# Buffers of a streamed transformer program at other address distances, and a longer warm-up

## The chip, the cores and the metric

One core of one Trainium2 chip runs the whole program in one launch. The metric is the device time of that core in microseconds (us), lower is better.

## The reference

A small language-model stack on 256 tokens of width 1024, batch 1. Block 1 has two layers. Each norms x, multiplies it with `w_in` (1024 x 8216 columns), runs four token mixers in parallel (retention, a state space scan, gated linear attention, an mLSTM), gates and merges their outputs, and projects with `w_out`. The first layer is followed by a gated feed-forward network, the second by a mixture of eight experts, two for each token:

```
u = h @ w_in;  y_ret, y_ssd, y_gla, y_ml = mixers(u)
merged = sum(sigmoid(gates) * einsum('bsnv,nvd->bsnd', ybr, w_branch)); x += merged @ w_out
ffn(h)  = (silu(h @ w1) * (h @ w3)) @ w2           # 1024 -> 2816 -> 1024
moe(h)  = sum over the two best experts e of gate_e * ffn_e(h)
```

Block 2 has two layers of attention beside a pooling branch, each with a modulated norm, followed by a modulated feed-forward network of the same size. Everything is float32.

## The kernel before, in words

Every product with a weight is done in three passes. A weight chunk of 128 x 2048 is loaded by one DMA issued by SP into a raw buffer; `chunk` splits it in halves of 1024 columns into a high part (`wh`, a cast on ScalarE, line 342) and a low part (`wl`, a subtraction on VectorE, line 338), both of type float32r. The activations are split the same way (`hh` and `hl`, `yh` and `yl`, and so on). `mm3` (lines 344 to 349) then issues high x high (line 346), low x high (347) and high x low (348). Most matmuls stream 256 columns (the tokens) through a stationary tile of 128 x 128 weights; in `tmode` and in the experts it is the other way round: 256 or 512 columns of weights stream through a stationary tile of tokens. In the profile a matmul is written out<-moving,stationary (`mm<-hh,wh`), where `mm` and `sm` are tags of PSUM banks. Before each matmul TensorE loads its stationary tile (PEld); while one matmul streams, the weights of the next are loaded.

The program has eight phases in this order, each with a work pool of its own: mix0 (work0), ff0 (work1), mix1 (work2), moe1 (work3), att0, ffb0, att1, ffb1 (work4 to work7). Three pools last through the program: `pers` (x, `hh`, `hl`, small things), `ring` (three raw buffers, four `wh`, four `wl`) and PSUM. Some phases have more weight buffers of their own, `rawx`, `whx` and `wlx`, which take turns with those of the ring. The order of instructions on each engine comes from the scheduler of the tile framework, which works from its own estimates, except where `in_order` and `after` fix it.

SBUF addresses follow from the program: pools stand one behind another (pers, ring, the phase's work pool), and within a pool the tags stand in the order of their first use, each with all its buffers, each buffer rounded up to 32 bytes per partition. The buffers that feed the three passes are 2048, 4096 or 8192 bytes long, and a tile of 128 columns is 512 bytes, so all tiles of a tag have one address modulo 512. These are, before:

| pool | address modulo 512 |
|---|---|
| pers, ring | hh, hl 256; raw, wh, wl 64; rstd 256 |
| work0, work2 | gate, m2, u 416; yh, yl 96 |
| work1 | unh, unl 64; yh, yl, whx, wlx 128 |
| work3 | G, xgh, xgl 288; mgh, mgl, whx, wlx 128; myh, myl 384 |
| work4, work6 | unh, unl 0 to 480 (buffers of 2064 bytes); whx, wlx 192 |
| work5, work7 | unh, unl 128 to 352 (2064 bytes); yh, yl, whx, wlx 448 |

At the start of `run` eight float32 matmuls of 128 columns on a tile of ones keep TensorE busy while the first loads are under way (lines 1605 to 1607). `settle` fills `hh` and `hl` some 25 us into the program; `ipad` and `rw` are small tiles of the mixers' phases. `cos2` and `sin2` in pers are first used late in moe1.

Of the kernel before, what the change touches and what calls it, by code (L numbers as in the profile page):

```python
# [17 lines left out]
P = 128  # L18
T = 256
# [18 lines left out]
# chunks of 256 columns of w_in, in the order of their use  # L38
# [4 lines left out]
class Layout:  # L43
    """Columns of a packed [128, n] array."""
# [50 lines left out]
def constants():  # L95
    """Tables that follow from the shapes alone."""
# [62 lines left out]
def host_arrays(i):  # L159
    """The inputs, laid out for the program: nothing is computed from them."""  # L160
# [48 lines left out]
    def kcols(w, width=256):  # L209
        """[1024, C] -> [C / width, 128, 8 * width]"""  # L210
        return w.reshape(KD, P, -1, width).transpose(2, 1, 0, 3).reshape(-1, P, KD * width)

    def krows(w, nk=2):
        """[K, 1024] -> [K / (128 nk), 128, nk * 1024]"""
        return w.reshape(-1, nk, P, D).transpose(0, 2, 1, 3).reshape(-1, P, nk * D)
# [27 lines left out]
    def mcols(w):  # L243
        """[8, 1024, 2816]: ten chunks of (4 k, 512) and one of (8 k, 256) for each expert."""
        a = w[:, :, :2560].reshape(NE, 2, 4, P, 5, 512).transpose(0, 4, 1, 3, 2, 5).reshape(NE, 10, P, 2048)
        b = w[:, :, 2560:].reshape(NE, 8, P, 256).transpose(0, 2, 1, 3).reshape(NE, 1, P, 2048)
        return np.concatenate([a, b], 1).reshape(NE * 11, P, 2048)
# [5 lines left out]

class Prog:
    def __init__(self, tc, a, out, stop=None):
        self.tc, self.nc, self.a, self.out, self.stop = tc, tc.nc, a, out, stop
        self.n = 0
        self.set, self.loaded, self.tabled, self.holds = None, None, [], []

# [1 line left out]
    def tile(self, pool, shape, tag, dt=F32, bufs=None):  # L261
        self.n += 1
        return pool.tile(list(shape), dt, tag=tag, name=f"{tag}_{self.n}", bufs=bufs)
# [24 lines left out]
    def group(self, name):  # L288
        """The activations from here on use this set of tables."""
# [17 lines left out]
    def wait(self, *ins, late=False):  # L307
        """These splits (or the like) are not to go before what is more urgent, on their engines."""
# [15 lines left out]
    def in_order(self):  # L324
        """VectorE and ScalarE take what is traced here in its order."""
# [14 lines left out]
    def split(self, hi, lo, src):  # L340
        """src = hi + lo, each in the 12 bits that one pass of TensorE carries."""
# [13 lines left out]
    def slot(self, tag, n, dt=F32, where=None):  # L355
        """The next buffer of a ring: BASE of them last through the program, more[tag] are the phase's own."""
# [9 lines left out]
    def chunk(self, src, n=2048, where=None, cuts=1, spare=None):  # L366
        """A chunk of weights [128, n] from DRAM, in two halves of (hi, lo); spare: gives buffers [128, 512] instead of the ring's."""
# [20 lines left out]
    def ahead(self, cuts=1):  # L388
        """The first two chunks of the next phase."""
        self.first = [self.chunk(q, where="base", cuts=cuts) for q in self.next]  # L390

    def kmajor(self, halves, width):
        """[(hi, lo)] by k-tile, of a chunk [128, k, width]."""
# [6 lines left out]
    def wmode(self, ps, ws, xh, xl, ncol=2, start=True, stop=True):  # L400
        """ps[c, t] (+)= sum over k of w[k, c] x[k, t]."""
# [6 lines left out]
    def tmode(self, ps, ws, xh, xl):  # L408
        """ps[t, c] = sum over k of x[k, t] w[k, c], for both blocks of tokens."""
# [6 lines left out]
    def small(self, shape, tag, bufs=2):  # L416
        """A buffer that may outlive a phase's own."""
        return self.tile(self.pers, shape, tag, F32, bufs)

    def square_sums(self, n, scale=None, tag="mm", add=None):  # L420
        """Sums over channels of squares, on all partitions, from n pairs of tiles [128, 512] given one after another."""
# [30 lines left out]
    def half(self, banks, k):  # L452
        """Tile k of the eight in four banks of PSUM."""
        return banks[k // 2][:, k % 2 * T:k % 2 * T + T]

    def begin(self, g, shift=None, fin=None, alias=False):
        """Norms x once its update has come, tile by tile, and starts with the two chunks that are already here.

        Their products are with x * g, before the scale r by token is known: whoever reads them applies it; with a
        shift, the products' column T is the product with the shift. fin: the gain of a norm of x itself that comes  # L460
        before."""
# [38 lines left out]
        for k in range(KD):  # L500
            for q in range(2):
                for i in self.raw_step(out[q], first[q], k):
                    if k == KD - 1:
                        # the sums of squares come first
# [9 lines left out]
    def places(self, tags, W):  # L514
        """Where the products of a chunk go: two tiles of W columns, in one bank if they fit."""
# [12 lines left out]
    def raw(self, chunk, *tags):  # L528
        """More products with x * g."""
# [6 lines left out]
    def settle(self, r, urgent=None):  # L536
        """The normed x as the rest of the phase takes it. urgent: what goes before the first chunk that follows, which goes before this."""
# [45 lines left out]
    def conv(self, ps, wname, bname, j0, pad, r=None):  # L583
        """silu of the causal convolution of two tiles of channels; taps in w columns (tile, tap). r: a scale by token."""
# [18 lines left out]
    def scores(self, h, k, q, ps):  # L603
        """ps[j, (i of block 0 and 1 | i of block 1)] = k_j . q_i for a head in half h % 2 of tile h // 2."""
# [5 lines left out]
    def values(self, po, h, v, s, tile=None, vs=None):  # L610
        """po[v, i] of a head: sum over j of v[j] s[j, i]."""
# [6 lines left out]
    def row(self, src, r, ps):  # L618
        """A row of src [128, 256] on all partitions."""
        self.nc.tensor.matmul(ps, self.ident[:, r:r + 1].to_broadcast([P, P]), src, start=True, stop=True)  # L620

    def seg(self, rows, r, colT, h):
        """exp(rows[r + h, i] + colT[j]) where j <= i, as [j, (i of both blocks | i of block 1)]."""
# [10 lines left out]
    def headnorm(self, o, g, gate, extra=None):  # L634
        """(head norm of o) * g * gate; o [128, 512] in PSUM. extra: added to the mean of the squares."""
# [27 lines left out]
    def gla(self, sm, gq, gk, l):  # L663
        """The decayed scores of the gated linear attention, [j, 4 heads, 384]."""
# [22 lines left out]
        # block 0 to block 1  # L687
# [10 lines left out]
        # halves of ever smaller blocks  # L698
# [27 lines left out]
        # each token with itself  # L726
# [9 lines left out]
    def mixers(self, l):  # L736
# [22 lines left out]
        # columns that pass a silu  # L759
# [12 lines left out]
        # rows by head, and the inputs of the linear attention  # L772
# [9 lines left out]
        # softplus(z) for dt, softplus(-z) for the forget gates: max(+-z, 0) + log1p(exp(-|z|))  # L782
# [23 lines left out]
        # -acs and i - B by key, for its own block and for the next  # L806
# [9 lines left out]
        # the stabilizer of the mLSTM: m = B + M  # L816
# [11 lines left out]
        # rows that go to all partitions: acs by head, -M by head  # L828
        rw = self.w([P, T], "rw", bufs=1)
# [3 lines left out]
        # gated linear attention  # L833
# [13 lines left out]
        # mLSTM  # L847
# [22 lines left out]
        # h = num / d, so that its norm is num / sqrt(mean num^2 + eps d^2)  # L870
        y_ml = self.headnorm(po, lambda t: self.par("mlg" + g, t), None, extra=d2)

        # state space
# [27 lines left out]
        # retention  # L901
# [29 lines left out]
        # gates and branches  # L931
# [20 lines left out]
        for i, (n, y) in enumerate(order[:3]):  # L952
            gates = []
            for dp in range(4):
                ps, gt = gate(n, dp)
                if i == 0:
                    # the sigmoid with the tables that are loaded: exp(-log(1 + exp(-x)))
# [25 lines left out]
        # the last one the other way round, so that the merged tiles come one after another  # L983
# [30 lines left out]
    def ffn(self, w1, w3, w2, begun, shifted=False, filler=0):  # L1014
        """(silu(h w1) * (h w3)) w2, in four banks of PSUM, two tiles of 128 columns in each."""
# [15 lines left out]
        for f in range(nfp):  # L1031
# [33 lines left out]
            # filler steps, evenly  # L1065
# [15 lines left out]
    def route(self, ps, rg):  # L1081
        """Ranks of the tokens in the lists of their experts, and their gates: [token, block, expert].

        ps: the logits, each still to be scaled by its token's rg[:, :, 0]; the gates go behind that."""
# [10 lines left out]
        # how many experts come before: with a larger logit, or with the same one and a smaller number  # L1095
# [16 lines left out]
        def rest():  # L1112
            """The gates, and how many tokens the fullest list has."""
# [25 lines left out]
    def gather(self, sel, rank, rg, iota, meanwhile=None):  # L1139
        """The tokens of the ranks in iota as columns, the way back, and their scales and gates, rg(block) by token."""  # L1140
# [17 lines left out]
        if meanwhile is not None:  # L1158
            # no weights before the tokens
# [53 lines left out]
    def gated(self, cx, py):  # L1213
        """The expert's output for its tokens, times their gates, split."""
# [8 lines left out]
    def scatter(self, cx, ys):  # L1223
        """x += ys, each row to its token."""
# [8 lines left out]
    def tokens(self, dp):  # L1233
        """Two tiles of the gained x by token, split; their part of the logits and of the sums of squares."""
# [42 lines left out]
    def moe(self):  # L1277
# [49 lines left out]
        # experts with more tokens than CAP: once more through all, for the tokens beyond  # L1327
# [15 lines left out]
    def rotary_tables(self):  # L1343
        """cos and sin of the positions, [channel, token]; 1 and 0 where nothing is rotated."""
# [7 lines left out]
        # ang modulo 2 pi, in two steps so that the multiples stay exact  # L1352
# [17 lines left out]
        # cos(a) = sin(pi / 2 - |a|)  # L1370
# [5 lines left out]
    def modulate(self, n, raw=None, junk=None):  # L1376
        """The next n of the 96 steps of c_act @ ada_w + ada_b, as columns: 8 for each of the six parts of a layer."""
# [10 lines left out]
    def post(self, acc, g, gate):  # L1388
        """x += gate * (norm of the columns in the banks acc) * g, tile by tile."""
# [19 lines left out]
    def attention(self, l, mod, cos, sin):  # L1409
# [13 lines left out]
        # q (heads t and t + 4 in tile t), k, v  # L1423
# [3 lines left out]
        def evac(ps, j, dst):  # L1427
            """Tile j of the products of w_in."""
# [26 lines left out]
        # scores [i, (j | j of block 0, j of block 1)] for the two blocks of i  # L1455
# [8 lines left out]
        def softmax(n):  # L1464
            """of the two heads of tile n."""
# [22 lines left out]
        def values(j):  # L1488
            """Tiles 4 + 2 j, 5 + 2 j of what w_out takes, from the four heads of tiles 2 j, 2 j + 1."""
            po = self.ps("sm")  # L1490
            for h in heads[4 * j:4 * j + 4]:
                pt = self.ps("sm")
                for q in range(3):
                    # to [j of block 0, i of both blocks | j of block 1, i of block 1]
# [8 lines left out]
        # u, with room for the windows, two groups at a time  # L1503
# [13 lines left out]
        def windows(j, eng):  # L1517
            u, *to = us[j]
            src = u
            for q in range(2 * j + 2):  # L1520
# [4 lines left out]
                # group q keeps its sum of w; the rest go on  # L1525
# [65 lines left out]
    def run(self):  # L1591
        from contextlib import ExitStack
        tc, nc = self.tc, self.nc
        with ExitStack() as ctx:
# [9 lines left out]
            # TensorE's clock rises while the first loads are under way  # L1604
# [137 lines left out]
```

## Time and profile before

| | us |
|---|---|
| median of 3 timed runs (2127.74 to 2129.61) | 2128.93 |
| span of the profiled execution, first to last instruction | 2128.1 |
| TensorE busy, share of the span | 2083.5, 98% |
| VectorE busy | 1697.6, 80% |
| ScalarE busy | 1321.0, 62% |

The profiled execution is one run of the program under the hardware profiler; its span is 0.8 us below the median of the timed runs. Busy times of TensorE are modelled at a matmul's end and overlap, so the time that a matmul costs is read from the distance of one start to the next, not from its busy time.

### The profile page before, as it was taken

The page shows a single profiled execution, that of the slowest core. Times are in us where ns is not written, and L with a number is a line of the kernel's source. Part 1 is how long each engine was busy: PE and PEld are TensorE (multiplying, and loading weights), DVE is VectorE, ACT ScalarE, POOL GpSimd, SP SyncE. Part 2 cuts the span into 40 slices and gives each one's busy share as a digit, 9 for nine tenths or more (in the row PEclk, how much of TensorE's full clock was granted, in tenths as well). Part 3 has the DMA queues.
Part 4 walks back from the last instruction along what each step waited for, and adds up shares of the span by engine and source line. Part 5 has one row for each costly group of instructions (what it writes and reads, how often), then busy time and mean ns, then how long its engine had stood idle before and what let it go on. Part 6 is the DMA issues. An engine that isn't in the chain of part 4 may idle for free. (4 is left out here: it accounts for less than half of the span.)

```text
span 2128.1 us, 35390 instructions
## 1 busy us (share of the span) xinstructions
PE 2083.5 (98%) x14172; PEld 1894.3 (89%) x14172; DVE 1697.6 (80%) x2315; ACT 1321.0 (62%) x1760; POOL 111.5 (5%) x111
## 2 busy tenths in 40 slices
PE   8999999999999999999999999999988999999997
PEld 8989999999889978888888888888877999989997
DVE  8868888658769688989888989889885988678653
ACT  6655554456555577777777777777765744557442
POOL 2000000010000150000000000000051000010000
PEclk9999999999999899999999999999999999999999
DMA  6526789635338778889898889898853598444640
GB/s 232 195 93 242 261 332 346 222 113 189 136 135 297 273 298 326 360 324 369 333 341 355 332 334 357 335 351 326 316 190 139 207 347 292 160 174 166 251 159 21
DMA packets 86171, 544.11 MB, mean 256 GB/s; under 512 B 10737, under 2 KB 11121, under 8 KB 27505
## 3 DMA queue, kind: packets, MB, share of 16 engines
q1 hardware_dynamic: 86000, 541.79, 67.8%
q8 instruction: 113, 1.85, 0.3%
q14 instruction: 58, 0.47, 0.1%
HBM read 540.67 MB, written 1.08 MB: 255 GB/s over the span
## 5 line engine op out<-in xcount | busy, mean ns | idle before, releaser
L342 ACT CAST wh<-raw 128x1024 fp32r<-128x1024 f32 (+1 forms) x328 | 336.9, 1040 | 252.2 <-PE mm L347 141.7
L338 DVE TENSOR_TENSOR wl<-raw,wh 128x1024 fp32r<-128x1024 f32 (+1 forms) x328 | 394.6, 1218 | 111.4 <-ACT wh L342 110.6
L338 DVE TENSOR_TENSOR wl<-rawx,wh 128x1024 fp32r<-128x1024 f32 x244 | 294.1, 1226 | 60.3 <-ACT wh L342 59.4
L342 ACT CAST wh<-rawx 128x1024 fp32r<-128x1024 f32 x244 | 252.3, 1048 | 118.3 <-PE mm L348 41.0
L338 DVE TENSOR_TENSOR wlx<-rawx,whx 128x1024 fp32r<-128x1024 f32 x198 | 240.1, 1227 | 70.4 <-ACT whx L342 62.1
L342 ACT CAST whx<-rawx 128x1024 fp32r<-128x1024 f32 x198 | 206.3, 1051 | 117.5 <-PE mm L348 30.4
L348 PE MATMUL mm<-hh,wl 128*128 128x256 f32 x800 | 226.2, 284 | 0.7 <-DVE wl L338 0.7
L346 PE MATMUL mm<-hh,wh 128*128 128x256 f32 x800 | 225.0, 283 | 1.7 <-ACT hh L301 1.0
L347 PE MATMUL mm<-hl,wh 128*128 128x256 f32 x800 | 226.1, 283 | 0.4 <-DVE hl L329 0.4
L338 DVE TENSOR_TENSOR wlx<-raw,whx 128x1024 fp32r<-128x1024 f32 x146 | 176.7, 1232 | 42.7 <-ACT whx L342 42.6
L342 ACT CAST whx<-raw 128x1024 fp32r<-128x1024 f32 x146 | 150.1, 1047 | 84.3 <-PE sm L347 26.9
L347 PE MATMUL mm<-wl,xgh 128*128 128x512 f32 (+1 forms) x446 | 170.0, 381 | 0.0
L346 PE MATMUL mm<-wh,xgh 128*128 128x512 f32 (+1 forms) x446 | 168.3, 380 | 0.0
L348 PE MATMUL mm<-wh,xgl 128*128 128x512 f32 (+1 forms) x446 | 168.0, 377 | 0.0
L347 PEld LDWEIGHTS mm<-hl,wh 128*128 128x128 f32 x800 | 152.1, 190 | 4.6 <-issue 3.7
L346 PEld LDWEIGHTS mm<-hh,wh 128*128 128x128 f32 x800 | 151.3, 190 | 5.2 <-issue 2.1
L348 PEld LDWEIGHTS mm<-hh,wl 128*128 128x128 f32 x800 | 151.5, 190 | 4.1 <-issue 2.3
L347 PE MATMUL mm<-wlx,xgh 128*128 128x512 f32 (+1 forms) x322 | 123.4, 383 | 1.4 <-DVE wlx L338 1.4
L346 PE MATMUL mm<-whx,xgh 128*128 128x512 f32 (+1 forms) x322 | 122.2, 382 | 0.0
L346 PE MATMUL sm<-hh,wh 128*128 128x256 f32 x440 | 121.8, 277 | 0.0
L347 PE MATMUL sm<-hl,wh 128*128 128x256 f32 x440 | 121.7, 277 | 0.0
L348 PE MATMUL sm<-hh,wl 128*128 128x256 f32 x440 | 121.6, 277 | 0.0
(438 smaller groups left out, 5792.6 us busy)
## 6 DMA issues: line engine op xcount, KB each, us to landing
rawx<-in_moe_dram SPq DMA_DIRECT2D x165, 1024.0 KB, 6.7
raw<-in_moe_dram SPq DMA_DIRECT2D x99, 1024.0 KB, 6.9
raw<-in_win_dram SPq DMA_DIRECT2D x66, 1024.0 KB, 4.9
ada<-in_ada_dram SPq DMA_DIRECT2D x72, 512.0 KB, 6.0
raw<-in_ffn_dram SPq DMA_DIRECT2D x17, 1024.0 KB, 6.9
rawx<-in_ffn_dram SPq DMA_DIRECT2D x16, 1024.0 KB, 6.7
S<-in_ada_dram SPq DMA_DIRECT2D x24, 512.0 KB, 4.7
raw<-in_wout_dram SPq DMA_DIRECT2D x12, 1024.0 KB, 4.9
```

Of the source, the lines that this page charges most:

```text
L338: return self.nc.vector.tensor_tensor(out, a, b, ALU.subtract)
L342: return self.nc.scalar.copy(hi, src), self.sub(lo, src, hi.bitcast(F32))
L346: i = m(out, lh, rh, start=start, stop=False, skip_group_check=True)
L347: m(out, lh, rl, start=False, stop=False, skip_group_check=True)
L348: m(out, ll, rh, start=False, stop=stop, skip_group_check=True)
```

## The change

`tile` puts a gap in front of the first use of nineteen tags, listed in `GAPS` by pool, tag and bytes per partition; nothing reads or writes a gap. `hh` and `hl` are allocated at the start of `run`, ahead of the other small tiles of pers. To make room, `rw` and `ipad` of the mixers' phases move from the work pool into the buffers of `sin2` and `cos2`. Behind the eight old warm-up matmuls 52 float32r matmuls are added, on ones in `hh` and `hl`: 36 of 256 columns (six at each of six distances) and 16 of 512 columns (four at each of four). Two GpSimd memsets fill what they read. All other edits in the diff take out comments.

```
+GAPS = (
+    ("pers", "hh", 192), ("ring", "raw", 320),
+    ("work0", "gate", 416), ("work2", "gate", 416), ("work0", "u", 320), ("work2", "u", 320),
+    ("work1", "unh", 256), ("work1", "yh", 448), ("work1", "whx", 256),
+    ("work3", "xgh", 32), ("work3", "mgh", 288), ("work3", "whx", 64), ("work3", "mgl", 448),
+    ("work4", "whx", 384), ("work6", "whx", 384),
+    ("work5", "yh", 384), ("work5", "whx", 256), ("work7", "yh", 384), ("work7", "whx", 256),
+)
     def tile(self, pool, shape, tag, dt=F32, bufs=None):
         self.n += 1
+        if pool is not self.psum and (pool.name, tag) in self.gaps:
+            free = self.gaps.pop((pool.name, tag))
+            pool.tile([P, free // 4], F32, tag=f"gap{self.n}", name=f"gap_{self.n}", bufs=1)
         return pool.tile(list(shape), dt, tag=tag, name=f"{tag}_{self.n}", bufs=bufs)
...
-        rw = self.w([P, T], "rw", bufs=1)
+        rw = self.tile(self.pers, [P, T], "sin2", bufs=1)
...
             for _ in range(8):
                 nc.tensor.matmul(ps[:, :P], self.ones, self.ones, start=True, stop=True)
+            moved, held = (self.tile(self.pers, [P, KD, T], n, F32R, 1).rearrange("p k t -> p (k t)") for n in ("hh", "hl"))
+            nc.gpsimd.memset(moved[:, :512].bitcast(F32), 1.0)
+            nc.gpsimd.memset(held[:, :256].bitcast(F32), 1.0)
+            for width, count, places in ((256, 6, (256, 96, 160, 224, 416, 480)), (512, 4, (256, 192, 64, 128))):
+                for d in places:
+                    w = (512 - d) // 4
+                    for _ in range(count):
+                        nc.tensor.matmul(ps[:, :width], held[:, w:w + P], moved[:, :width], start=True, stop=True)
...
-        self.ipad = self.w([P, T], "ipad", bufs=1)
+        self.ipad = self.tile(self.pers, [P, T], "cos2", bufs=1)
```

## Rows read from the trace of the kernel before

**Rows 1.** The page, part 1: busy us, share of the span, instructions.
```profile
PE 2083.5 (98%) x14172; PEld 1894.3 (89%) x14172; DVE 1697.6 (80%) x2315; ACT 1321.0 (62%) x1760; POOL 111.5 (5%) x111
```
**Rows 2.** Stages ff0 and ffb0: PE, PEld, DVE, ACT, POOL busy (count), clock, DMA share, GB/s.
```profile
307.00:462.00 155.00, 155.00 (x1324) 155.00 (x1323) 110.73 (x134) 69.09 (x80) 1.43 (x2) 1.00 0.68 253
1662.00:1840.00 178.00, 177.93 (x1514) 177.49 (x1512) 144.81 (x197) 89.65 (x113) 0.36 (x5) 1.00 0.79 290
```
**Rows 3.** Groups of matmuls by line and shape: count | busy us, mean ns | idle before.
```profile
L346 PE MATMUL mm<-hh,wh 128*128 128x256 f32 x800 | 225.0, 283 | 1.7 <-ACT hh L301 1.0 <-ACT wh L342 0.7
L346 PE MATMUL sm<-hh,wh 128*128 128x256 f32 x440 | 121.8, 277 | 0.0
L346 PE MATMUL mm<-yh,whx 128*128 128x256 f32 x264 | 73.8, 283 | 0.0
...
L346 PE MATMUL mm<-wh,xgh 128*128 128x512 f32 x366 | 145.8, 401 | 0.0
```
**Rows 4.** Stretches of 256-column matmuls, PE alone: us, PE busy (count), clock, DMA share, GB/s.
```profile
37.82:67.08 29.26, 29.26 (x260) 1.00 0.61 214
487.50:517.88 30.38, 30.38 (x259) 1.00 0.60 209
...
1826.65:1838.05 11.40, 11.40 (x97) 1.00 0.73 279
263.15:273.70 10.55, 10.55 (x90) 1.00 0.76 278
1908.78:1919.73 10.95, 10.95 (x94) 1.00 0.70 274
424.86:433.39 8.53, 8.53 (x74) 1.00 0.00 1
2086.92:2092.62 5.70, 5.70 (x50) 1.00 0.00 0
217.84:229.04 11.20, 11.20 (x99) 1.00 0.82 307
1536.61:1541.86 5.25, 5.25 (x47) 1.00 0.01 3
67.19:77.96 10.77, 10.77 (x98) 1.00 0.45 164
1731.60:1742.79 11.19, 11.19 (x97) 1.00 0.88 308
286.92:295.40 8.48, 8.48 (x74) 1.00 0.51 211
471.32:486.44 15.12, 15.12 (x129) 1.00 0.40 139
```
**Rows 5.** The same view for stretches of 512-column matmuls in the experts.
```profile
756.26:761.86 5.60, 5.60 (x26) 1.00 0.87 322
936.08:941.45 5.37, 5.37 (x25) 1.00 0.69 250
1541.99:1546.10 4.11, 4.11 (x20) 1.00 0.00 0
858.07:862.28 4.21, 4.21 (x20) 1.00 1.01 420
```
**Rows 6.** The start in order of time: start us, us, engine line op, tiles, count.
```profile
0.81 0.56 POOL L1668 MEMSET gkt<- 128x256 f32 x2
1.07 3.78 PE L1607 MATMUL mm<-ones 128*128 128x128 f32 x16 [1.07 <-DVE eps L1621]
...
6.19 0.39 PE L346 MATMUL sm<-gate,wh 128*128 128x256 f32 x1 [1.35 <-ACT wh L342]
...
13.28 0.50 PE L346 MATMUL sm<-gate,wh 128*128 128x256 f32 x2 [1.37 <-ACT gate L301]
```
**Rows 7.** Columns as in rows 2, for the first stretch with idle time after the start.
```profile
35.00:40.00 5.00, 3.83 (x31) 3.43 (x31) 5.00 (x9) 3.01 (x4) 0.00 (x0) 1.00 0.00 0
```

More of the change, by code (lines that the diff above doesn't have):

```diff
@@ L258, in __init__ @@
         self.set, self.loaded, self.tabled, self.holds = None, None, [], []
+        self.gaps = {(pool, tag): free for pool, tag, free in GAPS}
     def tile(self, pool, shape, tag, dt=F32, bufs=None):
         self.n += 1
+        if pool is not self.psum and (pool.name, tag) in self.gaps:
+            free = self.gaps.pop((pool.name, tag))
+            pool.tile([P, free // 4], F32, tag=f"gap{self.n}", name=f"gap_{self.n}", bufs=1)
         return pool.tile(list(shape), dt, tag=tag, name=f"{tag}_{self.n}", bufs=bufs)
```

## The prediction

> **What bounds the kernel now.** I read the page's part 1 first: TensorE is busy for 98% of the span, VectorE for 80% [rows 1]. Then the busy table by stage: in ff0, 1,324 matmuls in 155.00 us without an idle moment, 117.1 ns each; in ffb0, 1,514 in 178.00 us, 117.6 ns each, at the full granted clock [rows 2]. 256 columns at 2.4 GHz take 106.7 ns. So TensorE's own pace sets the end in the long stages, and what a change does to the distance between two starts goes into the time one for one there. The groups by line say how often each operand pair occurs (each row stands for three, one a pass): 3,720 matmuls `hh,wh`, 792 `yh,whx`, 1,098 `wh,xgh` of 512 columns [rows 3]. Last, I cut the table by stretches in which one operand pair runs without a break; width over count (less the one to three counted at the edges, which run on from before) is the pace of that pair [rows 4, 5].
>
> **What the distance does in this trace.** By distance I mean the address of the moving operand less that of the weights that load meanwhile (those of the next matmul), modulo 512, from the table of addresses. The stretches, in the order of [rows 4]:
>
> - 192: 258 matmuls in 29.26 us, 113.4 ns; in the second layer the same 258 take 30.38 us, 117.8 ns.
> - 0: 95 in 11.40 us, 120.0 ns; another pair, in another pool, 88 in 10.55 us, 119.9 ns.
> - 64: 93 in 10.95 us, 117.7 ns.
> - 128 and 384: 72 in 8.53 us, 118.5 ns, and 48 in 5.70 us, 118.8 ns. No DMA ran in either, so it isn't traffic.
> - 32 and 288: 96 in 11.20 us, 116.7 ns, and 45 in 5.25 us, 116.7 ns.
> - 320: 95 in 10.77 us, 113.4 ns, and 95 in 11.19 us, 117.8 ns.
> - 448: 72 in 8.48 us, 117.8 ns. 352: 126 in 15.12 us, 120.0 ns.
>
> So distance matters, by up to 6%, and two readings count. First, the odd multiples of 64 share two levels, 113.4 and 117.8, and keep whichever a stretch starts in. Secondly, distances 256 apart go alike: 32 with 288 (116.7, 116.7), 64 with 320 (117.7, 117.8), 128 with 384 (118.5, 118.8), and 192 with 448 on the slow level. Distances 128 apart don't: 0 gives 120.0 and 128 gives 118.5; 352 gives 120.0 and 480 or 224 is hardly seen. The pattern repeats every 256 bytes, as far as this trace shows it. No stretch of before runs at 256 itself.
>
> **Part 1: the gaps.** In pers, x and ones end at 128; with 192 bytes `hh` and `hl` stand at 320. The 192 and ring's own 320 add up to 512, so raw, `wh` and `wl` stay at 64 and the work pools begin where they did, modulo 512. In work0 and work2 `ipad` (1024 bytes) is gone and 416 + 416 gives 320 for `gate` and `m2`; `u` comes to 128, `yh` (96 - 288, with `rw`'s 1024 gone) to 320. In work1 `unh` 320, `yh` 320, `whx` 64. In work3 `xgh` 320, `mgh` and `mgl` 448, `whx` 0, `myh` 192, and `rstd` 448. In work4 to work7 `whx` 64, `yh` 320. Hence nearly every matmul of 256 columns goes to distance 256 (320 - 64, or 64 - 320). The exceptions are `gate,u` and `whx,xgh`, which go to 192, and those of 258 columns in block 2, where eight different offsets mix already.
>
> What 256 gives is the whole question. Bounds: 113.4 and 120.0 ns, the fastest and slowest levels of [rows 4]. I take 119.8, the mean at distance 0 with the first matmuls of each stretch, because 0 is the distance 256 away. The sum, with the starts of all consecutive matmuls sorted by distance (intervals under 128 ns; [rows 4] holds the first or longest stretch of each class):
>
> - 192 to 256: 3,580 intervals, mean 114.6 (seven in ten on the fast level): 3,580 x 5.1 ns = +18.3 us.
> - 320 to 256 (`hh,whx` in ffb0 and ffb1, `wh,hh`): 1,139, mean 116.2: +4.0 us.
> - 64 to 256: 614, mean 117.6: +1.4. 32 and 288 to 256: 588, mean 116.9: +1.7. 128 and 384 to 256: 992, mean 118.8: +1.0.
> - 352 to 256 (`gate,wh`): 560 at 119.9, nothing. 0 to 256 (`yh,whx` and others): 975, nothing.
> - To 192: `gate,u` from 0 and `whx,xgh` from 352, some 255 that gain 4.3 ns: -1.1 us.
>
> Together +25 us; with the bounds instead, from -30 us (all at 113.4) to +26 us.
>
> The matmuls of 512 columns [rows 5]: at 288 24 in 5.60 us, 233.3 ns; at 448 23 in 5.37 us, 233.5; at 0 18 in 4.11 us, 228.3; at 352 18 in 4.21 us, 233.9. `wh,xgh` goes from 288 to 256, for which I again take the value of 0, 229.5 on the mean: 1,002 x -3.4 ns = -3.4 us. `whx,xgh` goes from 352 to 192, like 448: nothing. `wh,mgh` goes from 448 to 128 and `whx,mgh` from 0 to 64, both unseen at this width in a long stretch; between 226.7 and 234 ns they are worth -4 to +2 us, and I take +1. Together -2.5 us, from -17 to +2.
>
> Net +22.5 us. Some of it falls into stages in which TensorE waits afterwards for a split or a norm: busy and span differ by 44.6 us [rows 1], and none of that lies in ff0, hardly any in ffb0. I let one tenth be absorbed: +20 us. VectorE and ScalarE only gain room, so nothing new comes late.
>
> The Trainium skill, "SBUF — State Buffer", section "Who interferes with whom", gives TensorE two independent read ports, one for the moving operand and one for the weights, and says that PE and ACT never wait on anyone. By that rule no distance would matter and part 1 would come to 0 us instead of +20. This trace disagrees: 113.4 against 120.0 ns at one clock and one shape [rows 4].
>
> **Part 2: `rw` and `ipad` in pers.** The same instructions on another buffer. The new neighbours in time, `cos2` and `sin2` of moe1, come hundreds of us after mix1's reads: nothing.
>
> **Part 3: the warm-up.** The old one ends at 4.85 us by its modelled end; the first real matmul starts at 6.19, held back by a cast of weights [rows 6]. GpSimd's two memsets (512 and 256 columns; two of 256 take 0.56 us [rows 6]) are some 0.8 us and are over before the old warm-up is. Then 36 x 118 ns and 16 x 231 ns are 7.9 us, a little more for the first ones if the clock is still at its low level: TensorE is free at about 12.8 us. The 24 matmuls that ran from 6.19 to about 11.7 us then need 2.9 us more, until 15.7, and the next one, which started at 13.28 when its token tile came [rows 6], is 2.4 us late. From there TensorE ran densely till about 35 us; the products of the first chunks release VectorE's scaling, which feeds `hh`, for which TensorE is idle for 1.2 us from 35 to 40 us [rows 7]. That wait hangs on the same late chain, so it covers little: +2 us. Bounds: nothing (all inside that wait and VectorE's own queue) and 8 us (all on the path).
>
> Sum: 2128.1 + 20 + 2 = 2150 us of span; the median of the runs is 0.8 us above the span now, so **2151 us**, 1.0% slower.
>
> **The rivals.**
>
> - Faster: 256 is as far as two operands can stand apart in 512 bytes, and if the pattern repeats every 512 and not every 256, it may be the distance at which the fast level is the only one. For it: 0 is the slowest of the multiples of 64 and 192 and 320, next to 256, the only ones seen on the fast level for long. Against it: the four pairs 256 apart. It decides as soon as 256 runs below 114.6 ns, the mean of the largest class. At 113.4 the 256-column part is -30 us and `wh,xgh` at 227 another -6; a quarter is lost to splits that now come late, with the warm-up -25 us: 2104 to 2106 us.
> - In between: 256 behaves like 128 and 384, the other even multiples, at 118.8 ns. For it: 0 may be special because both operands begin in the same place. The sum falls from +25 to +15, the net to +12: 2142 us.
> - No effect: the levels come from the order and the stage and the distance only goes along with them; the two layers of mixers at 192, one fast and one slow, speak for it; 0 at 120.0 and 119.9 in two pools and two stages [rows 4] speaks against it. Then only the warm-up counts: 2131 us. The port rule of the Trainium skill, weighed above, would give the same.
>
> **How the numbers follow.** The forecast has a chance of 0.6, its own range is 2142 to 2159 us; the in-between case 0.1; no effect 0.07; faster 0.23. A change under 0.2%, 4 us, can't be told from none in this kernel. Faster holds the fast rival and a little of the case without effect, 0.24; within 0.2% is the rest of that, 0.06; slower 0.70. The range runs from 2105 to 2160: below lies half of the fast case, above a warm-up that costs all its time.
>
> **What would show it.** In the changed trace: stretches of `hh,wh` in the mixers and in ff0 at 120 ns and not at 113.4 or 117.8, in both layers alike; ff0's 1,324 matmuls in some 158.5 us instead of 155.0; `wh,xgh` of 512 columns at 227 to 231; `gate,u` at 113.4 or 117.8; the first real matmul near 12.8 us. The six new matmuls at 256 among the warm-up should settle towards 120. I am wrong if `hh,wh` runs at or below 114.6 ns on the mean.

## The result, and the profile after

The changed kernel takes 2153.15 us (median of 4 runs, 2151.17 to 2155.26) against 2128.93 before: a ratio of 1.0112, interval 1.0100 to 1.0125. It is slower by 1.1%; the forecast was 2151. The profiled execution has a span of 2149.1 us, 21.0 more than before, at the same mean granted clock of 0.99.

Part 1 of the page of the changed kernel, to hold against [rows 1]:

```profile
PE 2108.1 (98%) x14224; PEld 1925.0 (90%) x14224; DVE 1699.0 (79%) x2315; ACT 1320.7 (61%) x1760; POOL 110.8 (5%) x113
```

TensorE alone has grown, by 24.6 us, some 8 of them for the 52 new matmuls; VectorE and ScalarE have the same work. The next view is the busy table of PE by stretches of the changed kernel, columns as in [rows 4]. The first stretch holds the same 1,322 matmuls as the ff0 row of [rows 2] (a count is two or three higher than the matmuls that begin in it), the second and third the `hh,wh` stretches of the two layers of mixers. Then the longest run at distance 256, `gate,u` at 192, and in the experts `wh,xgh` at 256, `whx,xgh` at 192, `wl,mgl` at 128 and `whx,mgh` at 64.

```profile
315.78:474.42 158.64, 158.64 (x1324) 1.00 0.67 249
38.90:69.98 31.08, 31.08 (x261) 1.00 0.57 208
500.00:530.83 30.83, 30.83 (x259) 1.00 0.59 209
...
291.91:481.74 189.83, 189.83 (x1584) 1.00 0.66 246
271.79:282.15 10.36, 10.36 (x90) 1.00 0.78 273
771.31:776.77 5.46, 5.46 (x26) 1.00 0.93 348
776.77:780.97 4.20, 4.20 (x20) 1.00 0.88 312
804.95:808.68 3.73, 3.73 (x17) 1.00 0.95 380
849.44:853.34 3.90, 3.90 (x19) 1.00 0.56 187
```

ff0 went from 155.00 to 158.64 us. Both layers of mixers run at 120.0 ns a matmul (259 in 31.08 us, 257 in 30.83), where before one ran at 113.4 and the other at 117.8 [rows 4]. The run from 291.91 on is 1,582 matmuls without a break at 120.0 ns: at 256 this trace has one pace. `gate,u` has 88 in 10.36 us, 117.7. With 512 columns the 24 at 256 take 227.5 ns, the 18 at 192 233.3, the 16 at 128 233.1 and the 17 at 64 229.4.

The start of the changed kernel, in order of time, against [rows 6]:

```profile
1.06 3.78 PE L1623 MATMUL mm<-ones 128*128 128x128 f32 x16 [1.06 <-DVE eps L1645]
4.50 8.35 PE L1631 MATMUL mm<-hh,hl 128*128 128x256 f32 x52
12.69 0.28 PE L362 MATMUL sm<-gate,wh 128*128 128x256 f32 x1
...
15.55 0.28 PE L362 MATMUL sm<-gate,wh 128*128 128x256 f32 x1
```

The 52 new matmuls hold TensorE to 12.7 us, and the matmul that began at 13.28 begins at 15.55, 2.3 us later.

### The profile page after: what moved, and what is told of

Its sections match the earlier page's. It is cut to its first block, busy times and chain, and to the rows that moved or that the text cites. A ratio compares the mean times of both kernels' runs of the same rounds, so it can differ in the third digit from the quotient of the medians.

```text
span 2149.1 us, 35509 instructions
## 1 busy us (share of the span) xinstructions
PE 2108.1 (98%) x14224; PEld 1925.0 (90%) x14224; DVE 1699.0 (79%) x2315; ACT 1320.7 (61%) x1760; POOL 110.8 (5%) x113
## 5 line engine op out<-in xcount | busy, mean ns | idle before, releaser
L358 ACT CAST wh<-rawx 128x1024 fp32r<-128x1024 f32 x244 | 252.2, 1048 | 115.5 <-PE mm L364 38.1
```

What stands on the lines that cost most here:

```text
L358: return self.nc.scalar.copy(hi, src), self.sub(lo, src, hi.bitcast(F32))
```

## Experiments

The theory: the pace of a matmul follows from how the address of the moving operand stands to that of the weights which load meanwhile, modulo 256 bytes, and 256 is the slow place of 256 columns. Rivals: the distances only go along with order and stage; the loss comes from the warm-up, or from many small moves; another engine is behind it.

### The distances alone, and the warm-up alone

`e1_no_warmup` takes the 52 matmuls and two memsets out of the changed kernel:

```
-            nc.gpsimd.memset(moved[:, :512].bitcast(F32), 1.0)
-            nc.gpsimd.memset(held[:, :256].bitcast(F32), 1.0)
-            for width, count, places in ((256, 6, (256, 96, 160, 224, 416, 480)), (512, 4, (256, 192, 64, 128))):
...
```

> The changed kernel without the 52 added matmuls and their two memsets; hh and hl stay where they are. Theory 1: the warm-up costs 2 us, so 2151 us against 2153 for the changed kernel, and the first real matmul starts near 6.2 us again. Rival: it costs nothing (2153), or all of its 8 us (2145).

2152.99 us, ratio to before 1.0101 (1.0086 to 1.0116).

`e2_warmup_only` keeps the warm-up and gives every buffer its distance of before (`rw` and `ipad` stay in pers, and the two memsets stay):

```
-GAPS = (
...
-)
+GAPS = (("pers", "hh", 128), ("ring", "raw", 384))
```

> The changed kernel with other gaps (128 bytes in front of hh, 384 in front of raw, no others), so that every distance is what it was before; rw and ipad stay in pers and the longer warm-up stays. Theory 1: the distances carry the loss, so 2131 us, 2 above before, with hh,wh on 113.4 or 117.8 ns again. Rival: the moved small buffers, the memsets or another order of the instructions carry part of it, and it stays clearly above 2133.

2130.75 us against 2130.92 for the kernel before on the same chip, ratio 1.0000 (0.9991 to 1.0009). ff0's 1,322 matmuls take the 155.0 us of before again:

```profile
307.67:462.70 155.03, 155.03 (x1325) 1.00 0.68 252
```

So the distances carry the loss, and the warm-up, with the moved `rw` and `ipad`, costs too little to be told from nothing. The order of the instructions does not explain it either. With the warm-up the scheduler gives another one (by the names of the tiles, TensorE's differs from that of before at 1,656 of 14,172 places), without it nearly the old one (32 places), and the loss is there in both orders with the changed distances and in neither with the old ones.

The stretch of [rows 7] shows some of what the warm-up does. First the changed kernel, then the one without warm-up, columns as there:

```profile
35.00:40.00 5.00, 5.00 (x44) 5.00 (x44) 5.00 (x11) 2.54 (x5) 0.00 (x0) 1.00 0.63 211
```
```profile
35.00:40.00 5.00, 3.35 (x26) 2.99 (x25) 5.00 (x8) 2.86 (x4) 0.00 (x0) 1.00 0.12 13
```

TensorE's wait of 1.65 us is there without the warm-up and gone with it. In the kernel before, the profile puts this wait down to the two parts of a weight chunk, `wh` from ScalarE and `wl` from VectorE:

```profile
36.62 0.39 PE L346 MATMUL mm<-hh,wh 128*128 128x256 f32 x1 [0.69 <-ACT wh L342]
37.60 0.39 PE L348 MATMUL mm<-hh,wl 128*128 128x256 f32 x1 [0.48 <-DVE wl L338]
```

In the order that comes with the warm-up ScalarE gets there sooner: it has written the last `hh` at 29.72 us, before at 32.31, and then casts a chunk ahead of four `u` activations that it did first before. So whether the late start or the other order ended the wait is not shown. Of two profiled runs with the same distances, the one with the warm-up alone comes to the first matmul of the ff0 row at 307.67 us and the one before at 307.00: some 0.7 us of the late start is left there.

### The largest step alone, forward and back

`e4_hh_256_alone` is the kernel with the warm-up alone, in which only `hh` and `hl` are moved, by 64 bytes, so that `hh,wh` goes from 192 to 256 (the other pairs with `hh` move by 64 as well, for which +1.6 us were expected):

```
-GAPS = (("pers", "hh", 128), ("ring", "raw", 384))
+GAPS = (("pers", "hh", 192), ("ring", "raw", 320))
```

> Of the change's gaps only the one ahead of hh and hl (and its counterpart ahead of the ring, so that the weights stay where they are): hh,wh and hl,wl go from 192 to 256, all else that does not use hh has its distances of before. Theory: 3,641 x (119.9 - 114.6 ns) = +19.3 us; hh,whx: 302 from 64 to 128 +0.3, 409 from 128 to 192 -1.8, 864 from 320 to 384 +2.1; wh,hh 276 from 320 to 256 +1.0; sum +20.9, 2151 from 2130, range 2147 to 2155. Rival (the loss comes from the many smaller moves together, this one is hidden by waits on other engines): under 2140.

2150.96 us, ratio 1.0102 (1.0087 to 1.0117). In its trace the 3,556 intervals of `hh,wh` and `hl,wl` have a mean of 119.8 ns (3,562 at 114.6 before); the `hh,wh` stretch of the first layer of mixers, 113.4 ns before, goes at 120.0:

```profile
38.78:69.74 30.96, 30.96 (x260) 1.00 0.56 212
```

The step that the forecast priced at +18.3 us is enough for nearly all of the loss.

`e3_hh_192` is the changed kernel with `hh` and `hl` put back, so that `hh,wh` and `hh,whx` are at 192 and all else stays as changed:

```
-    ("pers", "hh", 192), ("ring", "raw", 320),
+    ("pers", "hh", 128), ("ring", "raw", 384),
```

> The changed kernel with hh and hl alone put back to address 256 modulo 512 (gaps of 128 and 384 instead of 192 and 320): hh,wh and hh,whx at distance 192, wh,hh at 320, all else as changed, so yh, gate and unh stay at 256. Theory 1: some 5,600 matmuls go from 119.9 to about 115.2 ns, -26 us, of which nine tenths reach the end: 2129 us. Rival: if the distance isn't the cause, 2153 us as before this edit.

2120.17 us, ratio 0.9947 (0.9932 to 0.9962): faster than before, and by more than I had worked out. Its trace shows the rest: `hh,whx`, which before stood at 64, 128 and 320 with 116.2 to 119.0 ns, is at 192 too and has a mean of 113.7 over 1,559 intervals, which is 5.4 us, and `wh,xgh` keeps the 4 us that the change gave it.

### Matmuls alone

`m1_table` leaves out the whole model: one moving tile, stationary tiles at 32 distances in steps of 16 bytes, 40 matmuls of 256 columns (18 of 512) at each, begun in six (four) ways.

```
+            for width, count, ways in ((256, 40, ((), (P,), (512,), (258,), (P, P), (P, 258))), ...):
+                for d in range(0, 512, 16):
...
+                            m(ps[:, :w], held[d], moved[:, :w], start=True, stop=True)
```

> This kernel leaves out the whole model and only measures: one moving tile (address 128 modulo 512) and 32 stationary tiles, one at each distance 0, 16, ..., 496; 40 matmuls of 256 columns at each distance, six times, each time behind other short matmuls that shift the phase, then 18 matmuls of 512 columns, four times. Theory 1 (the pattern repeats every 256 bytes): 256 settles at 120.0 ns as 0 does, and each distance d runs like d + 256: 64, 192, 320 and 448 at 113.4 or 117.8, 128 and 384 at 118.5 to 118.8, 32 and 288 at 116.7, 96 and 352 at 120. Theory 2 (every 512, the weights and the stage of the program matter): 256 differs from 0, or the levels of the program don't come back here, where weights are the same tile over and over. Theory 3 (distance does not act): one level at all distances.

PE by stretches of that run, 24 matmuls each: distances 0, 32, 64, 64 (begun otherwise), 128, 192 and 192 (begun otherwise), then 256, 288, 320 twice, 384 and 448 twice; the last three are 9 matmuls of 512 columns at 0, 256 and 192.

```profile
6.26:9.14 2.88, 2.88 (x27) 1.00 0.59 225
65.28:68.08 2.80, 2.80 (x26) 1.00 0.00 0
123.19:126.02 2.83, 2.83 (x26) 1.00 0.00 0
147.61:150.33 2.72, 2.72 (x26) 1.00 0.02 6
240.85:243.70 2.85, 2.85 (x26) 1.00 0.00 0
358.48:361.20 2.72, 2.72 (x27) 1.00 0.00 0
363.19:366.01 2.82, 2.82 (x26) 1.00 0.00 0
475.34:478.22 2.88, 2.88 (x27) 1.00 0.00 0
534.36:537.16 2.80, 2.80 (x26) 1.00 0.00 0
592.27:595.10 2.83, 2.83 (x26) 1.00 0.00 0
616.69:619.41 2.72, 2.72 (x26) 1.00 0.00 0
...
709.93:712.78 2.85, 2.85 (x26) 1.00 0.03 6
827.56:830.28 2.72, 2.72 (x27) 1.00 0.00 0
832.27:835.09 2.82, 2.82 (x26) 1.00 0.03 6
944.46:946.50 2.04, 2.04 (x11) 1.00 0.00 0
1219.11:1221.15 2.04, 2.04 (x11) 1.00 0.00 0
...
1150.13:1152.23 2.10, 2.10 (x11) 1.00 0.00 0
```

The second half repeats the first: 120.0, 116.7, 117.8 or 113.3, 118.7, 113.3 or 117.8. After the first 20 us no other engine runs, and the DMA share is nothing in most rows, so the order, the stages and the traffic of the model are not needed: the distance modulo 256 gives the paces of [rows 4]. In this run only the address of the weights varies; that the distance counts, and not that address, is seen in `e4_hh_256_alone`, where the weights stayed and `hh` moved. At 192 and 448 four of six runs go at 113.3, at 64 and 320 one of six: how a stretch begins chooses, and it keeps its pace. With 512 columns the order is another: 0 and 256 are best (226.7), 192 has 233.

### All at the best distance of the table

`b1_all_192` puts all other 256-column pairs at 192 as well:

```
+    ("work0", "gate", 352), ("work2", "gate", 352), ("work0", "u", 320), ("work2", "u", 320),
+    ("work1", "unh", 192), ("work1", "yh", 448), ("work1", "whx", 320),
...
+    ("work5", "yh", 320), ("work5", "whx", 320), ("work7", "yh", 320), ("work7", "whx", 320),
```

> All pairs of 256 columns at distance 192: beside hh,wh and hh,whx now yh, unh, gate and m2 over wh, wl, whx, wlx too (some 2,740 matmuls that stood at 256 in the kernel with hh back). The 512-column pairs stay where the change put them. Theory (the pace of a matmul is set by its own distance): 2,740 x (119.7 - 114.5 ns) = 14 us less than the 2120 of that kernel, 2106, range 2102 to 2111. Rival (the two paces of distance 192, 113.3 and 117.8 ns, settle on the slow one in these stretches): 2,740 x 2 ns = 5 us less, 2115. Rival (VectorE and ScalarE, which make the split weights, become the bound once TensorE is this fast): 2120, no change from the kernel with hh back.

2123.44 us, ratio 0.9971 (0.9958 to 0.9983): not faster than with a third of the pairs at 256 (2120.17 us, ratio 0.9947). The theory missed by 17 us. Two long runs at 192 in this kernel, ff0 (1,322 matmuls) and a run in ffb0 (1,391):

```profile
307.90:457.73 149.83, 149.83 (x1325) 1.00 0.70 263
...
1666.15:1829.98 163.83, 163.83 (x1393) 1.00 0.81 302
```

The first goes at 113.3 ns, the second at 117.8 from end to end. Cut into twelves, the runs at 192 hold 206 at 113.3, 428 at 117.8 and 12 between, with `hh` back 302, 78 and 40; in neither is a twelve at 117.8 followed by one at 113.3. With `hh` back, each of the nine `hh` runs of ff0 follows `yh` at 256; each begins about 121, 122, 116, 114, 113 ns and settles at 113.3. That fits slow stretches which other distances end, and with one distance throughout few come between; no run shows this by itself. A price for each distance, at any rate, is not the whole theory.

`b2_both` adds the 512-column pairs at 0 or 256:

```
-    ("work3", "xgh", 32), ("work3", "mgh", 288), ("work3", "whx", 64), ("work3", "mgl", 448),
+    ("work3", "xgh", 32), ("work3", "mgh", 160), ("work3", "whx", 256),
```

> As the one with all 256-column pairs at 192, and all 512-column pairs at distance 0 or 256: whx,xgh 782 x (233.2 - 229.0) = 3.4 us less, wh,mgh 573 x (232.0 - 229.0) = 1.7 us less, whx,mgh 443 x (230.4 - 229.0) = 0.6 us less; 134 matmuls of 256 columns (whx,xgh) go from 115.3 to 119.3, 0.5 us more. Theory: 5 us less than the kernel with all at 192, 2101, range 2096 to 2107. Rival (in the expert stage the splits on VectorE and ScalarE hold TensorE, so that the 512-column pace hides): no difference to it, 2106.

2112.73 us, ratio 0.9922 (0.9908 to 0.9935), 11 us less than the one before it where 5 were expected: at 256 the 2,482 intervals now have a mean of 227.5 ns, and not the 229 of a kernel in which they alternate with other distances.

### What leaves the slow pace

`m2_pairs` alternates two distances, with one moving tile:

```
+                for p, q in ((0, 192), (0, 64), (64, 192), (352, 192), (32, 0), (288, 128)):
+                    for _ in range(30):
+                        go(p, w)
+                        go(q, w)
...
```

> Matmuls alone, all of the model left out. One moving tile; the stationary tiles alternate between two distances (P Q P Q, and P P Q Q). Theory (a matmul is slowed by the load that runs under it, that of the next matmul's weights): in P P Q Q with P at 0 and Q at 192, the interval of the matmul whose successor holds Q is the short one (113 to 118 ns) and the one whose successor holds P the long one (120 ns), whatever it holds itself. Rival (its own weights' address decides): the other way round, the matmul that holds Q is short. In P Q P Q the two theories differ by one place in each pair. The 258-column matmuls at 16 distances: theory, the same pattern as 256 columns, about 1 ns longer each. Runs of 32 matmuls at 192, 448, 64 and 320 after one to three others: if how a run starts decides which of the two paces it keeps, both 113.3 and 117.8 appear at each of these four distances and stay to the end of the run.

Neither theory held for all pairs. With 0, 0, 64, 64 the four intervals were 119, 121, 113 and 113 ns, as the rival has it. But with 0, 0, 192, 192 the four intervals were 120, 118, 118 and 117 or 118 ns; with 352 and 192 in turn they were 125 and 115. The price isn't that of one distance, whichever of the two weights it is taken to, and it does not add. But 64 and 192 in turn, in ones or in twos, went at 113.3 throughout. At 258 columns all 16 distances lie between 116.7 and 123.3 ns, most at 120. Of stretches of 32, 30 of 48 settled at 113.3 at 192 (the same ones at 448) and 7 of 48 at 64 (the same at 320), the rest at 117.8.

From this came `b3_lo_128`: as `b2_both`, with the low parts that move (`hl`, `yl`, `unl`, `m2`) 128 bytes further on, so that of each three matmuls two are at 192 and one is at 320. `m3_two_one` ran groups of three alone, two at P and one at Q, again with one moving tile.

```
+    ("pers", "hh", 128), ("pers", "hl", 128), ("ring", "raw", 256),
...
```
```
+                            go(p, 256, 2)
+                            go(q, 256)
```

> The kernel with all 256-column pairs at 192 and the 512-column pairs at 0 or 256, with one thing more: the low parts that move (hl, yl, unl, m2) stand 128 bytes further on, so that of each three matmuls two are at distance 192 and one is at 320. At 192 throughout that kernel had two paces, 113.3 ns in 196 and 117.8 ns in 437 of its stretches of twelve matmuls, and a stretch kept its pace once it had it. In the run of matmuls alone every mix of 64 and 192 went at 113.3. Theory (a mix of 192 and 320 leaves the slow pace within a few matmuls): 8,000 matmuls x (116.4 - 113.4 ns) = 24 us less than 2113, 2089, range 2085 to 2095. Rival (the mix has the same two paces, chosen by how a run begins): about 2113, range 2103 to 2119.

> Matmuls alone, the model left out. Groups of three matmuls of 256 columns, two at distance P and one at distance Q, in runs of 36, each run begun in four ways (for P, Q = 192, 64 and 192, 192 in eight more). Theory: P = 192 with Q = 64 goes at 113.3 ns however it begins, and P = Q = 192 at 113.3 or 117.8 by how it begins. Rival: both show two paces. With Q at 0, 96 or 112, where the table of single distances has 120, one of three matmuls is slow: theory of one price for each distance (113.3 + 113.3 + 120) / 3 = 115.5 ns; if the paces of neighbours interact, some other value.

Alone, 192 with 64 was at 113.3 in all 12 starts, and 192 throughout in four of 12. But the kernel came to 2128.68 us (ratio 0.9988, 0.9979 to 0.9997), 16 us above `b2_both` (14 by the ratios), and its ff0 stands here:

```profile
311.26:466.96 155.70, 155.70 (x1324) 1.00 0.69 251
```

117.8 ns on the mean, in six intervals that repeat, each within 1 ns: 118, 118, 115, 118, 117, 120 in the first matmuls, 115, 122, 117, 118, 117, 118 in most of the stretch. And 192 with one in three at 0, 96 or 112 went at 117.8 alone, where adding prices gives 115.5. One thing that differed between kernel and run alone was that in the kernel the moving tile moved, and in the run the weights. `m4_high_low` varies both in the order of the three passes: the low part stands dm bytes from the high one, the second weights ds bytes from the first.

```
+                for mv, o, st, q in ((high, 0, first, s), (low, dm // 4, first, s), (high, 0, second, t)):
+                    m(ps[:, :w], st[:, q:q + P], mv[:, o:o + w], start=True, stop=True)
```

> Matmuls alone, the model left out, in the order of its three passes: high part over the first weights, low part over the first weights, high part over the second weights. The low part stands dm bytes away from the high one, the second weights ds bytes from the first (0 to 224 in steps of 32, modulo 256), from a distance of 192 or 64, each of 64 pairs begun in three ways; 512 columns from 0 and 64, begun in one. In the kernel with the low parts 128 bytes on (dm = 128, ds = 0) the three intervals were 118, 118, 115 and 118, 117, 120 (117.8 on the mean); in the run of matmuls alone where the weights moved (dm = 0, ds = 128) the same mix of distances gave 113.3. Theory (a load of weights runs under the ends of two moving streams, so that where both streams stand counts, not one distance): dm = 128 with ds = 0 gives 117.8 here too, dm = 0 with ds = 128 gives 113.3 in all three starts. Rival (a mix is a mix, and the model's kernel lost its 4.5 ns to something else, as traffic of VectorE and ScalarE on the weights): both give 113.3 here. For 512 columns from 0: 226.7 at dm = ds = 0; with one of them 128, over 229.

PE by stretches of 24 matmuls from 192: three starts with dm = ds = 0, three with ds = 128, three with dm = 128.

```profile
6.03:8.75 2.72, 2.72 (x27) 1.00 0.77 291
10.40:13.22 2.82, 2.82 (x26) 1.00 0.02 6
14.86:17.58 2.72, 2.72 (x26) 1.00 0.00 0
59.67:62.39 2.72, 2.72 (x26) 1.00 0.00 0
64.01:66.73 2.72, 2.72 (x27) 1.00 0.00 0
68.37:71.09 2.72, 2.72 (x26) 1.00 0.00 0
436.90:439.73 2.83, 2.83 (x27) 1.00 0.02 6
441.37:444.19 2.82, 2.82 (x26) 1.00 0.00 0
445.85:448.68 2.83, 2.83 (x27) 1.00 0.00 0
```

113.3, 117.8, 113.3; then 113.3 three times; then 117.8 three times, with the kernel's first row of six in two starts and its second in the third. So the model's traffic is not needed for it. Of the 64 pairs of dm and ds, dm = 0 with ds = 128 is the only one at 113.3 from either base in all starts. That fits a load that runs under the ends of two moving streams, but no run here shows when a load reads. Matmuls of 512 columns from 0 went at 227.3 ns with dm = ds = 0, 228.9 with dm = 128 and 231.3 with ds = 128.

`b4_wl_128` applies it: `b2_both` with `wl` (and `wlx` outside the experts) 128 bytes further on.

```
+    ("pers", "hh", 128), ("ring", "raw", 384), ("ring", "wl", 128),
...
+    ("work1", "unh", 64), ("work1", "yh", 448), ("work1", "whx", 320), ("work1", "wlx", 128),
...
```

> The kernel with all 256-column pairs at 192 and the 512-column pairs at 0 or 256; in it now the second weights of each three passes (wl, and wlx outside the expert stage) stand 128 bytes further on, modulo 256, than the first ones, and nothing that moves is shifted: of three matmuls two are at distance 192 and one at 64. In the run of matmuls alone this order (dm = 0, ds = 128) went at 113.3 ns in all three starts, where 192 throughout had 113.3 and 117.8. In the expert stage the moving wl of the ring is 128 off (dm = 128, ds = 0 for 512 columns: 228.9 against 226.7). Theory: 8,000 x (116.4 - 113.4 ns) = 24 us less than 2113, and 1,560 of 512 columns x 2 ns = 3 us more: 2092, range 2087 to 2098. Rival (the loads and casts of the model disturb the fast pace, as in the kernel with the low parts shifted): 2113 or more. Rival (another engine bounds before): 2100 to 2113, with idle time on TensorE put down to VectorE or ScalarE.

2099.57 us (2098.07 to 2101.54), ratio 0.9856 (0.9842 to 0.9869): 1.4% faster than before. ff0 (at 113.3 ns already in `b1_all_192` and `b2_both`), then the second layer of mixers, which took 117.8 ns or more in every kernel so far, and the run in ffb0, which took 117.8 in those two:

```profile
305.34:455.16 149.82, 149.82 (x1324) 1.00 0.71 262
480.34:509.48 29.14, 29.14 (x259) 1.00 0.62 214
...
1653.62:1811.28 157.66, 157.66 (x1393) 1.00 0.85 314
```

All three go at 113.3 to 113.4 ns; the 8,167 intervals at 192 and 64 have a mean of 113.6. It missed the expected 2092 by 8 us, and from one profiled run to the other the starts of all matmuls say where (13.2 us less of span): 22.3 us gained at 256 columns, 4.7 lost at 512 (`wl,xgl` and `wl,mgl` at 128: 233.5 against 227.3, where the run alone had 228.9), and 4.0 lost to matmuls that now wait, about half of it for a weight split. From the page's groups, `b2_both` first:

```profile
L364 PE MATMUL mm<-hh,wl 128*128 128x256 f32 x800 | 226.7, 285 | 0.5 <-DVE wl L354 0.5
```
```profile
L365 PE MATMUL mm<-hh,wl 128*128 128x256 f32 x800 | 225.4, 283 | 2.6 <-DVE wl L355 2.5
```

## Why the prediction was right

- **256 acts like 0.** It does: 119.9 ns over 8,493 intervals (119.8 taken), ff0 in 158.64 us (158.5 forecast). What carried the forecast past the rival "256 is best" were the four pairs 256 apart in [rows 4], and the run of matmuls alone shows the repetition at all sixteen.
- **The sum at 256 columns.** By the same classes, with what the changed trace shows: 192 to 256 +18.9 us (+18.3 forecast), 320 +4.2 (+4.0), 64 +1.4, 32 and 288 +1.8, 128 and 384 +1.1, to 192 -0.8 (-1.1, as `gate,u` fell on 117.8). With 0.1 for what came from 0, +26.7 against +25.
- **The sum at 512 columns.** `wh,xgh` 1,002 x (228.9 - 232.9 ns) = -4.0 us (-3.4 forecast); `wh,mgh` -0.7 and `whx,mgh` +0.5, together -0.2 where I took +1. In all some -4.2 against -2.5: this term was mis-sized, by a little under 2 us.
- **The tenth that waits take back, and the warm-up.** I let a tenth, 2.3 us, be absorbed by waits. TensorE's idle time, span less busy, is 44.6 us before and 44.4 in the profiled run without the warm-up (2153.7 less 2109.3), so next to nothing was; the timed runs of that kernel, 22.1 us above before and good to about 3, can't tell the two apart. And I put +2 on the warm-up, because I held that the wait of [rows 7] is one for `hh`, hangs on the same late chain and covers little. The profile puts it down to a weight chunk, the instructions stand in another order with the warm-up, and the wait is gone; the warm-up alone measures -0.2 us, within about 2. Both steps were off by some 2 us, in opposite directions, and that the total came out so near is partly luck.
- **Two sums that decide nothing.** By the prediction's own counts, all of 256 columns at 113.4 ns give some -28.5 us and not -30, and the in-between case at 118.8 ns gives +17 and not +15, which is 2144 us and not 2142.
- **No effect.** The rule of the Trainium skill ("SBUF — State Buffer", section "Who interferes with whom") that TensorE's two read ports are independent would make this kernel and the one before alike but for the warm-up. With TensorE alone at work, matmuls of 256 columns took 113.3 to 120.0 ns at the distances of [rows 4]; the measurement decides against the rule for these float32r matmuls. Whether it is at these ports that the two operands meet is not shown.
- **What the prediction had not seen.** It read the two levels at 192 as a fixed share, seven in ten fast. In the runs at one distance a stretch kept its pace, and `hh` runs that followed `yh` at 256 settled at 113.3. That fits how little was gained by putting everything at the best distance, but what ends a slow stretch was not tested by itself.

## What to carry to other kernels

Where TensorE's pace sets the end, cut the busy table into stretches of one operand pair and divide width by count: two paces for one shape at one clock can mean that placement counts, and moving a buffer by 64 bytes can be worth 1%. Time the pair alone in the order of the real passes before moving buffers, because a table of single distances did not carry over to mixed ones. And look at how often the good pace occurs, not only whether it does.

## What the runs showed of the hardware that was not expected

- 256 columns of float32r: by distance modulo 256, 120.0 ns at 0, 96, 112 and 144, 116.7 at 48, 118.3 at 224 and 240, and two lasting paces, 113.3 and 117.8, at 64 and 192. 208 reached 123.3 in two of six starts.
- 512 columns: 226.7 ns at 0, 228.9 at 64, 230 to 234.2 at most others. The best place for one width is among the slowest for the other.
- Two weights of a pair 128 bytes apart end the slow pace at 192 (113.3 in all starts, in a run alone and in the model); two moving tiles 128 apart force it (117.8). Why is open.
